# Splits of peer_u between the HGRN heads' steps, modulation rows as products on TensorE, one-hot gate products in fp32

## The chip, the core and the metric

The kernel runs on one core of one Trainium2 chip. A core has TensorE (PE in the rows, its weight loads PEld), VectorE (DVE), ScalarE (ACT), GpSimd (POOL) and SyncE (SP), whose queue issues most of the transfers, and 16 DMA engines. Each engine executes its own queue in order. The metric is the device time of one execution in microseconds. Of the kernel before, three executions took 3266.9 to 3286.5 us, their median is 3282.34 us.

## The reference

One layer over 1024 latent tokens of width 1024 and 256 context tokens. Two linear-attention mixers of four heads each run in both directions over the sequence (HGRN2 with a gate per key channel, mLSTM with a stabilised exponential gate); their output goes through a projection, a residual and a layer norm, then through PEER: eight heads of product-key retrieval over 128 x 128 = 16384 experts of one neuron each. Cut to what the change touches:

```python
mod_l = jax.nn.silu(c) @ w_mod[l] + b_mod[l]                 # 6 x 1024 modulation values
sh1_l, sc1_l, g1_l, sh2_l, sc2_l, g2_l = jnp.split(mod_l[:, None, :], 6, axis=-1)
...
x = _affine_ln(ALPHA * x + g1_l * (mix_l @ w_out[l]), ln1_g[l], ln1_b[l])
h = _modulate(x, sh2_l, sc2_l)
# PEER, per token: the gates of its 8 x 16 best experts, idx = key0 * 128 + key1
act = gelu(jnp.einsum('pd,ped->pe', h, u_tab[idx]))
y = jnp.einsum('pe,ped->pd', gate * act, v_tab[idx])
x = _affine_ln(ALPHA * x + g2_l * y, ln2_g[l], ln2_b[l])
```

## The kernel before

The kernel is one program in stages. A scheduler puts the instructions of each engine in an order by its own model of their durations; the code's order is only the starting point, so an instruction written in one stage may stand in an earlier one, as far as buffers allow. In order of time:

- **0 to 85 us**: the modulation columns of the first layer norm, the layer norm, and its transposed output `xmT` as a pair of fp16 and bf16 (a value and its remainder). All large products are three passes of such pairs.
- **85 to 550 us, HGRN** (`hgrn`): gates of the mLSTM, the values `v`, then four heads in two directions, eight calls of `one()`. One call projects the gate (`sg`, `kr`), makes a scan on VectorE (L398), decayed keys and queries (`kh`, `kt`, `qt`, `qe`), transposes `kh` into `km` through the PSUM tile `tr` (L428; `tr` has two buffers), and then makes the states `S` chunk by chunk (L449, L451) and the outputs. In the same stretch `modrows` makes four rows of 1024 modulation values that are wanted later: for each of 11 blocks of 384 columns, eight loads `wm` of w_mod and a multiply (L682) or multiply-add (L684) on VectorE, 128 partitions wide; the sums over the partitions are left to `modsums` (L697, a product with ones, after the last head).
- **550 to 950 us, mLSTM** and the readout: VectorE carries convolutions (L550, L552) and decay matrices (L615).
- **950 to 1157 us, mix_out**: output projection, layer norm, the query projection for part of the tokens.
- **1157 to 1490 us**: scores against the keys and top-k.
- **1490 to 2003 us, gate tiles**: five tiles of 128 tokens (640 tokens, the "dense" ones) get a matrix of 16384 gates per token, by products of one-hot rows, in 160 quads of four tokens each (`gate_tile`, L1045 to L1056).
- **2003 to 3275 us, final stage**: for each of 128 second keys, `dense_s` takes the product of all 640 tokens with 128 experts' u rows (L1147), `dense_w` applies gelu and gates, `dense_y` multiplies with the v rows (L1180). The other three tiles of tokens gather their experts' rows by indirect transfers (`Gather`, L1088), with a VectorE dot product (L1107) or accumulation (L1115) for each row; these run beside all stages from 1157 on.

Two things tie the stages. **Splits**: `peer_u`, transposed, is needed as a pair of fp16 or bf16 value and remainder. `g.uprep(m)` makes m of the 128 parts: SP loads 512 KB into `us` (L195), ScalarE casts it (L198), GpSimd subtracts (L199), SP stores 512 KB to the DRAM tile `Ud` (L202). They are spread over the stages as filling; `us` and `uT` have two buffers each. **Spilled tiles**: `dense_s` of 60 of the 128 parts (`NPRE`) is done ahead, in the scoring and gate stages, and its result goes to DRAM (`Sd`, 320 KB) and is loaded again in the final stage.

## Time and profile before

| what | value |
| --- | --- |
| median of three runs | 3282.34 us |
| profiled execution: time, span | 3277.14 us, 3275.3 us |
[...]
| busy share: PE, DVE, POOL, ACT | 90%, 86%, 57%, 38% |
| chain that ended last: PE, DVE, DMA, issue | 38%, 32%, 13%, 9% |
| HBM traffic | 274 GB/s over the span |

The profile is of one execution. A busy share is a mean over all stages, so it tells which engine leads but not what a stage waits for; the rows below give it by stage. The chain that ended last is followed back from the last instruction, at each step to what released it; a line's share there is the time that it held the end up. "issue" is time in which the engine waited for nothing that the profile shows. In a row such as `uT<-us,uT 128x1024 x7` the output stands left of the arrow.

### The profile page before, as it was taken

What the parts mean: (1) busy time and instruction counts of PE and PEld (TensorE: products, weight loads), DVE (VectorE), ACT (ScalarE), POOL (GpSimd) and SP (SyncE); (2) the same over time, 40 slices, a digit from 0 to 9 for tenths busy, and PEclk for the clock granted to TensorE, in tenths of its full rate; (3) what the DMA queues carried; (4) which work ended last, traced back from release to release, by engine and by line L of the source; (5) the groups of instructions that cost most, each with busy time, mean ns of one, the idle gap of its engine ahead of it and who ended that gap; (6) DMA issues with size and microseconds to landing.
All of it is one profiled execution on the core that took longest, in us unless ns stands there. A gap on an engine that the chain in (4) does not pass through costs nothing.

```text
span 3275.3 us, 51376 instructions
## 1 busy us (share of the span) xinstructions
PE 2947.6 (90%) x18685; PEld 1911.1 (58%) x18831; DVE 2821.4 (86%) x5605; ACT 1231.1 (38%) x1869; POOL 1853.5 (57%) x1358
## 2 busy tenths in 40 slices
PE   7888789787889889999999987999999999999997
PEld 3644456465777666667777764555555555555553
DVE  8478774889878999999998887889998999889999
ACT  3464462334435442226667663212222122222222
POOL 3555563552236636535555665666676666666665
PEclk8888887898999999999999987999999999999998
DMA  7676664651147659876889789999999999999994
GB/s 287 223 249 224 219 223 160 208 185 52 46 158 253 227 202 351 299 288 213 286 276 309 260 265 363 342 338 362 359 341 365 355 361 360 370 365 360 359 357 181
DMA packets 328626, 900.63 MB, mean 275 GB/s; under 512 B 29084, under 2 KB 121252, under 8 KB 320436
## 3 DMA queue, kind: packets, MB, share of 16 engines
q1 hardware_dynamic: 217780, 494.64, 42.8%
q0 software_dynamic: 110592, 402.70, 33.8%
q8 instruction: 147, 2.41, 0.3%
q14 instruction: 107, 0.88, 0.1%
HBM read 758.80 MB, written 138.43 MB: 274 GB/s over the span
## 4 chain that ended last, share of the span: by engine, by line
PE 38%; DVE 32%; DMA 13%; issue 9%; POOL 4%; ACT 3%; SPq 0%; DVEq 0%; POOLq 0%; ACTq 0%
PE y L1180 14%; PE S L1147 12%; DMA row<-in_peer_v_dram,idx 3%; DVE us L1107 3%; DVE mz L552 2%; PE pj L230 2%; DVE hg L1115 2%; DMA row<-in_peer_u_dram,idx 2%; DMA us<-in_peer_ut_dram 2%; DMA uT<-Ud 2%; DVE mra L684 2%; PE y L1054 2%; PE y L1055 2%; POOL row L1088 1%; DMA wm<-in_w_mod_dram 1%
## 5 line engine op out<-in xcount | busy, mean ns | idle before, releaser
L1147 PE MATMUL S<-hTd,uT 128*128 128x320 f16 (+1 forms) x6144 | 912.7, 303 | 19.7 <-DMA uT<-Ud 11.1
L1180 PE MATMUL y<-vs,w 128*128 128x512 bf16 x3726 | 860.7, 380 | 21.8 <-DVE ya L1187 7.7
L1147 PEld LDWEIGHTS <-uT 128*128 128x128 bf16 x6144 | 608.5, 99 | 292.3 <-DMA uT<-Ud 14.6
L1180 PEld LDWEIGHTS <-w 128*128 128x128 bf16 x3840 | 376.0, 98 | 441.8 <-issue 23.0
L1088 POOL DMA_INDIRECT row<-in_peer_u_dram,idx x384 | 389.4, 1014 | 269.0 <-DVE us L1107 136.9
L1115 DVE SCALAR_TENSOR_TENSOR hg<-row,dot,hg 128x1024 f32<-128x1024 f32 x381 | 488.5, 1282 | 35.5 <-DMA row<-in_peer_v_dram,idx 32.2
L1088 POOL DMA_INDIRECT row<-in_peer_v_dram,idx x384 | 397.2, 1034 | 208.9 <-DVE hg L1115 103.6
L1107 DVE SCALAR_TENSOR_TENSOR us<-row,hg 128x1024 f32<-128x1024 f32 x384 | 465.0, 1211 | 40.4 <-DMA row<-in_peer_u_dram,idx 36.4
L199 POOL TENSOR_TENSOR uT<-us,uT 128x1024 bf16<-128x1024 f32 x128 | 305.8, 2394 | 254.5 <-ACT uT L198 226.3
L1152 ACT ACTIVATE ge<-S 128x320 f32<-128x320 f32 x256 | 114.0, 446 | 546.5 <-PE S L1147 544.9
L222 PE MATMUL pj<-xmT,wb 128*128 128x512 f16 (+3 forms) x1216 | 270.2, 377 | 30.0 <-ACT pad L542 19.8
L1046 POOL TENSOR_TENSOR kT<-kT,eT 128x512 bf16<-128x512 bf16 x160 | 176.3, 1115 | 207.5 <-DVE kT L1045 118.0
L1163 POOL TENSOR_TENSOR vs<-row,vs 128x1024 bf16<-128x1024 f32 x128 | 274.0, 2141 | 33.4 <-ACT vs L1162 31.0
L1162 ACT CAST vs<-row 128x1024 bf16<-128x1024 f32 x128 | 133.4, 1043 | 339.6 <-DMA row<-in_peer_v_dram 327.5
L230 PE MATMUL pj<-wb,xmT 128*128 128x256 f16 (+1 forms) x1728 | 227.3, 291 | 26.2 <-DVE rsg L755 16.6
L1187 DVE TENSOR_TENSOR ya<-ya,y 128x512 f32<-128x512 f32 x310 | 207.8, 680 | 27.6 <-PE y L1180 26.7
L230 PEld LDWEIGHTS <-xmT 128*128 128x128 f16 (+1 forms) x1968 | 187.2, 104 | 75.4 <-issue 34.3
L222 PEld LDWEIGHTS <-wb 128*128 128x128 f16 (+1 forms) x1248 | 127.1, 104 | 153.6 <-issue 52.4
L198 ACT CAST uT<-us 128x1024 bf16<-128x1024 f32 x128 | 132.9, 1043 | 189.2 <-DMA us<-in_peer_ut_dram 177.4
L1054 PE MATMUL y<-kT 128*128 128x128 bf16 x640 | 159.5, 295 | 31.2 <-DVE kT L1047 22.5
L1050 ACT ACTIVATE kT<-kT,gf 128x128 bf16<-128x128 bf16 x320 | 148.7, 570 | 98.5 <-PE y L1054 56.9
L1056 ACT COPY gst<-y 128x512 f32<-128x512 f32 x160 | 178.3, 1123 | 11.6 <-PE y L1055 11.6
(399 smaller groups left out, 4408.6 us busy)
## 6 DMA issues: line engine op xcount, KB each, us to landing
us<-in_peer_ut_dram SPq DMA_DIRECT2D x128, 512.0 KB, 5.2
Ud<-uT SPq DMA_DIRECT2D x128, 512.0 KB, 2.9
uT<-Ud SPq DMA_DIRECT2D x128, 512.0 KB, 7.0
row<-in_peer_v_dram SPq DMA_DIRECT2D x128, 512.0 KB, 7.1
Gd<-gst SPq DMA_DIRECT2D x20, 1984.0 KB, 13.6
Gt<-Gd SPq DMA_DIRECT2D x31, 1280.0 KB, 11.2
Sd<-ge SPq DMA_DIRECT2D x60, 320.0 KB, 8.8
kT<-Sd SPq DMA_DIRECT2D x60, 320.0 KB, 8.7
```

Source lines behind the costliest of these rows:

```text
L199: nc.gpsimd.tensor_tensor(lo, uf, hi, op=OP.subtract)
L222: g.nc.tensor.matmul(ps[:, :t1 - t0], w.t[a][:, k, c0:c0 + 128], g.xmT[b][:, k, t0:t1], start=(k == 0 and a == b), stop=(k == KD - 1 and a ...
L230: g.nc.tensor.matmul(ps, g.xmT[a][:, k, t * 128:(t + 1) * 128], w.t[b][:, k, :w.n], start=(k == 0 and a == b), stop=(k == KD - 1 and a == 1))
L1054: nc.tensor.matmul(o, oh[:, 2, :, i], oh[:, 0, :, i], start=True, stop=False)
L1056: nc.scalar.copy(gs[:, :, q * 4:q * 4 + 4].rearrange("p e t -> p t e"), ps.rearrange("p (t e) -> p t e", e=128))
L1088: d = g.nc.gpsimd.indirect_dma_start(out=b, out_offset=None, in_=self.I["peer_u" if n < 128 else "peer_v"][0], in_offset=bass.IndirectOffs ...
L1107: nc.vector.scalar_tensor_tensor(g.gscr, b, 1.0, self.ps, op0=OP.mult, op1=OP.mult, accum_out=dot[:, j:j + 1])
L1115: nc.vector.scalar_tensor_tensor(self.ps, b, dot[:, j:j + 1], self.ps, op0=OP.mult, op1=OP.add)
L1147: m = nc.tensor.matmul(ps[:, :hn], uT[:, a, k, :], g.hTd[b][:, k, i * hn:(i + 1) * hn], start=(k == 0 and (a, b) == (0, 0)), stop=(k == KD ...
L1163: nc.gpsimd.tensor_tensor(v[:, 1], vf, v[:, 0], op=OP.subtract)
L1180: nc.tensor.matmul(ps, w[:, a, t * 128:(t + 1) * 128], v[:, b, h * 512:(h + 1) * 512], start=(n == 0), stop=(n == 3 * GI - 1))
L1187: nc.vector.tensor_add(ya, ya, ps)
```

## The change

Four parts.

1. **Splits.** The calls of `g.uprep` move: none is left in the mLSTM, its readout and after the heads; 8 stand after each of the two blocks of HGRN values, and 10 inside each `one()` (3 between the gate projections, 3 between the transposes, 4 between the states). 32 stay in mix_out. `uT` gets a third buffer.
2. **Modulation rows.** VectorE's multiplications and `modsums` go. The rows are now products on TensorE, with the conditioning column `cs` as the stationary operand and 512 columns of w_mod streaming: one row of output each, in four different quarters (32 partitions) of the PSUM tile `tr`, in two halves of four rows. The loads `wm` are 32 of 512 KB. A `tr` buffer is held until its half is summed.
3. **Buffers of the last stages.** `score` takes its staging from `us` in place of `uf`; `dense_s` has three `uT` buffers; the dot product L1107 writes its unused product over its own input row.
4. **Gate tiles.** A quad had two compares, a VectorE, a GpSimd and two ScalarE multiplications in bf16, and eight bf16 products on operands with a step of four elements. It now has two compares, a GpSimd multiplication into fp32, written 512 bytes apart from element to element, a ScalarE copy into fp32, and four fp32 products on contiguous operands. `NPRE` rises from 60 to 66.

```diff
@@ Uprep
-            uT = self.pool.tile([128, 2, KD, 128], BF, name="uT")
+            uT = self.pool.tile([128, 2, KD, 128], BF, name="uT", bufs=3)
@@ hgrn
         inputs(0)
+        g.uprep(8)
         inputs(1)
+        g.uprep(8)
...
                 nc.scalar.activation(kr[:, t0:t1], ps, AF.Sigmoid, scale=-1.0)
+                g.uprep(1)
...
                 nc.scalar.copy(km[:, t0:t0 + n, :], pt[:, :n * 128].rearrange("p (t k) -> p t k", k=128))
+                g.uprep(1)
...
                         states(4 + 8 * n + 4 * (i // 2 if d == 0 else 1 - i // 2))
+                        g.uprep(1)
...
                     one(2 * hh + e, d, w, qs[e])
-                    g.uprep(4)
@@ modrows
-            for k in range(KD):
-                wt = mp.tile([128, CW], F32, name="wm", bufs=2)[:, 0:n]
...
-                nc.vector.scalar_tensor_tensor(acc, wt, g.cs[:, k:k + 1], acc, op0=OP.mult, op1=OP.add)
+    for h in range(2):
+        bb = mp.tile([128, 512], F32, name="bb")
...
+        ps = g.pp.tile([128, 512], F32, name="tr", bufs=2)
         for k in range(KD):
+            for x in range(2):
+                wt = mp.tile([128, 1024], F32, name="wm", bufs=2)
+                c = 2 * D + h * 2048 + x * 1024
+                nc.sync.dma_start(wt, I["w_mod"][0, k * 128:(k + 1) * 128, c:c + 1024])
+                for i in range(2):
+                    q = 2 * x + i
+                    nc.tensor.matmul(ps[32 * q:32 * q + 1], g.cs[:, k:k + 1], wt[:, i * 512:(i + 1) * 512],
+                                     start=(k == 0), stop=(k == KD - 1))
+        for q in range(4):
...
+            nc.vector.scalar_tensor_tensor(bb[o], ps[o], 1.0 if r == 2 else 0.0, bb[o], op0=OP.add, op1=OP.add)
+            nc.sync.dma_start(g.mrow[r:r + 1, (n % 2) * 512:(n % 2 + 1) * 512], bb[o])
@@ gate_tile
-            nc.vector.tensor_tensor(oh[:, 1], g.iob, col(0), op=OP.is_equal)
-            nc.gpsimd.tensor_tensor(oh[:, 3], oh[:, 1], col(3), op=OP.mult)
-            nc.vector.tensor_tensor(oh[:, 0], g.iob, col(1), op=OP.is_equal)
-            nc.vector.tensor_tensor(oh[:, 2, :, 2:], oh[:, 1, :, 2:], col(2)[:, :, 2:], op=OP.mult)
-            for i in range(2):
-                nc.scalar.activation(oh[:, 2, :, i], oh[:, 1, :, i], AF.Copy, scale=gf[:, t0 + i:t0 + i + 1])
+            for a in range(2):
+                nc.vector.tensor_tensor(cm[:, a], g.iob, eT[:, a, None, t0:t0 + 4].to_broadcast([128, 128, 4]), op=OP.is_equal)
+            nc.gpsimd.tensor_tensor(oh[:, 0].rearrange("p t e -> p e t"), cm[:, 0], gf[:, None, t0:t0 + 4].to_broadcast([128, 128, 4]), op=OP.mult)
+            nc.scalar.copy(oh[:, 1], cm[:, 1].rearrange("p e t -> p t e"))
...
-                nc.tensor.matmul(o, oh[:, 2, :, i], oh[:, 0, :, i], start=True, stop=False)
-                nc.tensor.matmul(o, oh[:, 3, :, i], oh[:, 0, :, i], start=False, stop=True)
+                nc.tensor.matmul(ps[:, i * 128:(i + 1) * 128], oh[:, 0, i], oh[:, 1, i], start=True, stop=True)
@@ Gather
-            nc.vector.scalar_tensor_tensor(g.gscr, b, 1.0, self.ps, op0=OP.mult, op1=OP.mult, accum_out=dot[:, j:j + 1])
+            nc.vector.scalar_tensor_tensor(b, b, 1.0, self.ps, op0=OP.mult, op1=OP.mult, accum_out=dot[:, j:j + 1])
@@ dense_s
-    uT = g.up.tile([128, 2, KD, 128], BF, name="uT")
+    uT = g.up.tile([128, 2, KD, 128], BF, name="uT", bufs=3)
@@ constants
-NPRE = 60
+NPRE = 66
```

How the scheduler's order changes is shown at three places. The first is GpSimd at the end of the HGRN and the start of the mLSTM: `qe` (L422, after the change L425) belongs to the last HGRN head, L77 splits weights of the mLSTM, `kw` is its first own operation. Before:

```order
L422 TENSOR_TENSOR qe<-q,qe 128x1024
L199 TENSOR_TENSOR uT<-us,uT 128x1024 x7
L77 TENSOR_TENSOR wb_4674<-wf,wb_4673 128x2048
L199 TENSOR_TENSOR uT<-us,uT 128x1024 x4
L77 TENSOR_TENSOR wb_5276<-wf,wb_5275 128x2048
L199 TENSOR_TENSOR uT<-us,uT 128x1024 x6
L77 TENSOR_TENSOR wb_5928<-wf,wb_5927 128x2048
L199 TENSOR_TENSOR uT<-us,uT 128x1024 x2
L586 TENSOR_TENSOR kw<-mkm,gcol 128x1280
L199 TENSOR_TENSOR uT<-us,uT 128x1024 x3
```

And with the change, at the same place:

```order
L425 TENSOR_TENSOR qe<-q,qe 128x1024
L199 TENSOR_TENSOR uT<-us,uT 128x1024 x10
L77 TENSOR_TENSOR wb_4787<-wf,wb_4786 128x2048
L199 TENSOR_TENSOR uT<-us,uT 128x1024 x4
L77 TENSOR_TENSOR wb_5293<-wf,wb_5292 128x2048
L199 TENSOR_TENSOR uT<-us,uT 128x1024 x6
L77 TENSOR_TENSOR wb_5873<-wf,wb_5872 128x2048
L589 TENSOR_TENSOR kw<-mkm,gcol 128x1280 x2
L647 TENSOR_TENSOR acm<-acm,tm 128x2x128 x2
```

72 splits stand ahead of this `qe` before and 76 after; behind it there were 28 up to the end of the mLSTM, nine of them behind the first `kw`, and now there are 20, all ahead of it.

The second place is the first HGRN heads. On VectorE, before (L398 is a head's scan, L406, L420, L421 and L419 its keys and queries, L468 the masked scores):

```order
L682 TENSOR_SCALAR mra<-wm,cs 128x384
L684 SCALAR_TENSOR_TENSOR mra<-wm,cs,mra 128x384 x3
L398 SCALAR_TENSOR_TENSOR sg<-rs,sg 128x1280
L406 TENSOR_TENSOR qt<-sg 128x1024
L684 SCALAR_TENSOR_TENSOR mra<-wm,cs,mra 128x384 x2
L420 SCALAR_TENSOR_TENSOR kt<-kr,oml,kt 128x1024
L421 TENSOR_TENSOR qt<-q,qt 128x1024
L684 SCALAR_TENSOR_TENSOR mra<-wm,cs,mra 128x384
L419 SCALAR_TENSOR_TENSOR kh<-kr,oml,kh 128x1280
```

With the change (L401, L409, L422 to L424 and L472 are the same steps, L404 the scan of a backward head, L453 the first state of a head):

```order
L401 SCALAR_TENSOR_TENSOR sg<-rs,sg 128x1280
L409 TENSOR_TENSOR qt<-sg 128x1024
L423 SCALAR_TENSOR_TENSOR kt<-kr,oml,kt 128x1024
L424 TENSOR_TENSOR qt<-q,qt 128x1024
L404 SCALAR_TENSOR_TENSOR sg<-rs,sg 128x1280
L409 TENSOR_TENSOR qt<-sg 128x1024
L692 SCALAR_TENSOR_TENSOR bb<-tr,bb 1x512 x4
L453 COPY S<-up 128x128
L455 SCALAR_TENSOR_TENSOR S<-S,dec,ob 128x128
```

The accumulations are gone from between the steps; three heads' scans and the four additions of the first half of the rows stand ahead of the first state. On TensorE, with the change, the products of the rows stand ahead of the first head's transposes (L431, `kh`), which are written into the PSUM buffer that the first half (`tr_989`) leaves; `pj_2800` is a gate projection:

```order
L222 MATMUL pj_2800<-xmT0_108,wb1_2471 128x512
L686 MATMUL tr_989<-wm_1046,cs_123 1x512 x2
L686 MATMUL tr_989<-wm_1050,cs_123 1x512 x2
L686 MATMUL tr_1067<-wm_1068,cs_123 1x512 x2
L431 MATMUL tr_2009<-ident_81,kh_1999 128x128 x4
L686 MATMUL tr_1067<-wm_1072,cs_123 1x512 x2
```

Before, a projection stood directly ahead of these transposes, and the gate projections of later heads behind them; now those of four heads stand ahead.

The third place is TensorE at the end of the gate tiles. Before, the last quads' products (L1054, L1055) follow each other, and the next dense tile (L1147) stands behind the last of them:

```order
L1055 LDWEIGHTS kT
L1055 MATMUL y<-kT 128x128
L1147 LDWEIGHTS uT
L1147 MATMUL S<-hTd_8036,uT 128x320
```

With the change the last quad (L1039) stands in the middle of a dense tile (L1131):

```order
L1131 LDWEIGHTS uT
L1131 MATMUL S<-hTd_7813,uT 128x320
L1039 MATMUL y<-kT 128x128 x8
L1131 LDWEIGHTS uT
L1131 MATMUL S<-hTd_7813,uT 128x320
L1131 LDWEIGHTS uT
L1131 MATMUL S<-hTd_7814,uT 128x320
```

In units of one dense tile, 26.5 stand ahead of the eighth quad before and 66.4 ahead of the first product of the final stage (L1180); with the change it is 27.7 and 71.0.

## Rows read from the trace of the kernel before

**Rows 1.** busy by stage: length, PE, PEld, DVE, ACT, POOL; PEclk, DMA share, GB/s

```profile
143.00:528.00 385.00, 321.93 (x1683) 194.91 (x1703) 269.40 (x301) 198.58 (x238) 221.36 (x96) 0.84 0.66 224
528.00:950.00 422.00, 339.95 (x2273) 247.65 (x2284) 344.09 (x707) 149.99 (x197) 149.86 (x64) 0.88 0.39 132
950.00:1157.00 207.00, 179.11 (x1367) 140.27 (x1366) 175.09 (x540) 99.77 (x157) 122.36 (x70) 0.95 0.67 230
1157.00:1490.00 333.00, 305.30 (x2273) 222.19 (x2273) 318.49 (x1439) 93.96 (x172) 149.37 (x150) 0.97 0.76 274
1490.00:1947.00 457.00, 431.25 (x3348) 344.36 (x3346) 411.78 (x961) 313.30 (x567) 274.74 (x255) 0.97 0.85 275
1947.00:1982.00 35.00, 17.91 (x124) 13.38 (x123) 32.74 (x55) 25.94 (x46) 27.39 (x26) 0.54 0.89 286
...
2003.00:3252.00 1249.00, 1231.47 (x6682) 665.36 (x6795) 1132.14 (x1395) 281.09 (x396) 832.07 (x658) 1.00 0.93 352
```

**Rows 2.** chain of waits by line, 85 to 550 us, 950 to 1157 us

```profile
by line: DVE mra L684 12.7%; issue 8.9%; DMA wm<-in_w_mod_dram 8.6%; DMA us<-in_peer_ut_dram 6.1%; PE oa L480 5.4%; PE pj L230 5.3%; PE pj L222 4.6%; PE oa L477 3.6%; PE ob L440 3.2%; DVE qt L406 3.1%; PE up L440 3.1%; DVE S L451 2.7%; PE s
...
by line: PE pj L842 13.8%; DMA us<-in_peer_ut_dram 12.1%; POOL uT L199 8.1%; issue 7.1%; DMA wqf<-in_peer_wq_dram 6.4%; DVE mz L851 3.9%; POOL uT L77 3.7%; PE oa L918 3.7%; DVE lnst L145 3.0%; DVE ind L889 2.6%; DVE cnt L951 2.6%; DVE mh L8
```

**Rows 3.** L199's subtractions by stretch: length, POOL busy (count), PEclk, DMA share, GB/s

```profile
0.00:85.00 85.00, 15.82 (x7) 0.87 0.76 288
85.00:200.00 115.00, 45.10 (x19) 0.92 0.68 237
200.00:528.00 328.00, 117.10 (x48) 0.83 0.63 214
528.00:750.00 222.00, 65.53 (x28) 0.87 0.55 186
```

**Rows 4.** timeline of SP's queue: two loads of splits, two splits apart

```profile
93.64 0.43 SPq L195 DMA_DIRECT2D us<-in_peer_ut_dram  x1
...
103.71 0.38 SPq L195 DMA_DIRECT2D us<-in_peer_ut_dram  x1
```

**Rows 5.** what SP's queue waited for, 157 to 530 us: us, times, longest

```profile
SPq L202 <- POOL uT L199: 80.3, 19, 18.0
...
SPq L680 <- DVE mra L684: 60.3, 35, 6.2
```

**Rows 6.** groups by line (second: 1490 to 1947 us): busy us, mean ns | idle before

```profile
L552 DVE SCALAR_TENSOR_TENSOR mz<-pad,cwT,mz 128x1024 f32<-128x1024 f32 x64 | 98.8, 1554 | 0.7
...
L1056 ACT COPY gst<-y 128x512 f32<-128x512 f32 x144 | 160.7, 1123 | 11.2 <-PE y L1055 11.1
```

**Rows 7.** pieces of the chain of waits: start us, us, what

```profile
549.88 0.95 PE tr L697 x2
...
2965.19 6.52 PE S L1147 x48
```

**Rows 8.** single lines: ns min/median/max, first and last start us, forms

```profile
L684 DVE SCALAR_TENSOR_TENSOR mra<-wm,cs,mra x77: 472/1454/4420, 164.9 to 466.3; 128x384 f32<-128x384 f32 x70, 128x256 f32<-128x256 f32 x7
...
L552 DVE SCALAR_TENSOR_TENSOR mz<-pad,cwT,mz x64: 1251/1277/5079, 592.8 to 810.5; 128x1024 f32<-128x1024 f32 x64
...
L428 PE MATMUL tr<-ident,kh x80: 272/273/475, 212.7 to 512.7; 128*128 128x128 f32 x80
...
L1046 POOL TENSOR_TENSOR kT<-kT,eT x160: 1032/1052/2162, 1491.8 to 1978.8; 128x512 bf16<-128x512 bf16 x160
...
L574 ACT COPY mkm<-tr x12: 363/574/599, 656.1 to 829.0; 128x512 f32<-128x512 f32 x8, 128x256 f32<-128x256 f32 x4
```

**Rows 9.** timeline of the gate stage: start us, us, engine, line

```profile
1702.76 0.29 PE L1054 MATMUL y<-kT 128*128 128x128 bf16 x1 [0.62 <-DVE kT L1048]
...
1703.02 0.40 DVE L1045 TENSOR_TENSOR kT<-iob,eT 128x512 bf16<-128x512 bf16 x1
...
1703.10 0.30 PE L1055 MATMUL y<-kT 128*128 128x128 bf16 x1
...
1703.77 1.35 DVE L1045 TENSOR_TENSOR kT<-iob,eT 128x512 bf16<-128x512 bf16 x1
```

## What is predicted, and why

> **What bounds the kernel now.** I read the table by stages first: in each stretch, which engine is busy nearly all the time? From 2003 us to the end it is TensorE, 1231 of 1249 us; while experts are scored (1157 to 1490) it is VectorE, 318 of 333; in the mLSTM no engine is full but VectorE leads with 344 of 422. The gate stage (1490 to 1947) has TensorE at 431 of 457, and then 56 us in which TensorE is busy for 26 [rows 1]. The HGRN stretch, 143 to 528, is nobody's: TensorE 322 of 385, VectorE 269, and its granted clock is 0.84 [rows 1]. So there I read the chain of waits by line: the accumulation of the modulation rows (L684) is its largest line with 12.7%, the loads `wm` behind it have 8.6%, the loads of the splits 6.1% [rows 2]. The splits run through all of it: 48 from 200 to 528, one per 6.8 us [rows 3]. When nothing is in their way two of them, on two `us` buffers, take 10.1 us, 5.0 each [rows 4]. What holds them back is the shared queue of SP: it stood 60 us waiting for L684 and 80 us for the subtractions of the splits [rows 5], and all later transfers stand behind it.
>
> **The change, part by part.** The profiled execution has a span of 3275.3 us and a time of 3277.1, 5 us under the median of 3282.3; the sum is made against 3277.1.
>
> *Modulation rows.* 77 accumulations, 112 us of VectorE at a median of 1.45 us, go [rows 8], with 11 first multiplies and 56 of 88 loads (the bytes stay the same). In their place TensorE takes 64 products of one output row by 512 columns. The trace has that shape in the old sums, 0.95 us for the two records of one [rows 7]: 61 us in all if they run one after the other; the four quarters of the array might overlap, which no row here shows, and at twice the speed it is 30. TensorE's 322 us become 352 to 383. The eight old sums stood on the chain one by one, 8 x 0.95 = 7.6 us, and go wholly: **-8**.
>
> *Splits to the HGRN heads.* The order on GpSimd shows that the planner had pulled most of them there already: 72 stand before the last head's `qe` now, 76 then. 26 (7 and 19) are through at 200 us [rows 3], so 50 must follow. At the undisturbed 5.2 us (the pair at 10.1 and a little for the weight splits) that takes 260 us, at today's 6.8 us 340, against 328: bounds -68 and +12. With L684 gone SP waits less, so the middle, 6.0, would give -28. But TensorE with 352 to 383 us must fit too, and it now has 63 us idle of 385; a stage of 365 us leaves it nearly none. I take **-20**.
>
> *mLSTM.* 20 splits instead of 28 fall here [rows 3], and all before the first `kw`. L552 shows what a split costs VectorE: 1277 ns at the median, 1554 in the mean [rows 6, 8], 64 x 0.28 = 18 us of stalls, since the two engines take turns. Eight of 28 fewer: 8/28 x 18 = **-5**. Nothing (all off the chain) and -18 (none left beside L552) are the bounds.
>
> *mix_out.* 32 splits instead of 28. The splits' loads and subtractions have 20% of the chain of this 207 us stretch [rows 1, 2], 42 us for 28, 1.5 each: 4 x 1.5 = **+6**. Hidden wholly it is 0, at full cadence 4 x 6.0 = +24.
>
> *Scoring.* One `us` buffer takes the place of two `uf`, and a third `uT` is there. VectorE at 318 of 333 us covers this: **0**. Writing the dot product back over `row` in place adds no element to L1107: 0, unless the gather that reuses the row comes later; it waits for L1107 today already.
>
> *Gate tiles.* A quad of tokens now has 3.17 us (457 over the 144 evacuations L1056 of that stretch [rows 6]). What goes per quad: one VectorE multiply, two ScalarE ones, and eight matmuls, of which three pitches take 0.34 us (1702.76 to 1703.10), 0.9 for eight [rows 9]. What comes: four fp32 products of 128 columns, each a quarter of the 0.95 us of one with 512 [rows 7], together 0.95; a ScalarE copy that reads with a step; and a GpSimd multiply that writes with a step of 512 bytes. For the copy the nearest rows are L574, 0.57 us contiguous, and L1056, 1.12 us writing with a step [rows 6, 8]. Two ScalarE instructions go for this one, and ScalarE, at 313 of 457, has room for either: 0. The multiply is 1.05 us now [rows 8] and I take it as unchanged, nearest to itself, the risk being the third rival. By the order 3.4 more dense tiles are made in this stage. One takes 6.52 us of TensorE for 48 of its products, nearly the tile [rows 7]: +22. TensorE is idle for 26 + 17 = 43 us from 1490 to 1982 [rows 1], much of it for handshakes of a quad that now has fewer of them. So the 22 fit in: **-5**, bounds -25 (half the idle time closed and no more work) and +60 (nothing closed, and the third `uT` brings loads earlier into a DMA share of 0.85).
>
> *Final stage.* 71.0 tiles of 128 stand before its first product in the order, 66.4 today: 4.6 fewer to make here, 4.6 x 6.52 = 30 us of a TensorE that is busy for 98.6% [rows 1, 7]. A spilled tile is read back as 320 KB where a made one reads 512, so DMA, at 0.93, doesn't grow. I take **-27**; 0 if transfers, at 0.93 [rows 1], set the pace instead.
>
> Sum: -8 - 20 - 5 + 6 + 0 - 5 - 27 = -59, so **3218 us**.
>
> **The rivals.** *First: the heads start late.* In the order all 16 products of the first half of the modulation rows, and its four additions, stand ahead of the first head's transposes and first state. Those transposes start at 212.7 us now and the eighth head's last one at 512.7, 43 us per head [rows 8]. The half needs 16 loads of 512 KB, on SP between some 14 splits: at 6.0 us from 165 us on, where the first accumulation is now [rows 8], they end near 250. The heads then start 38 us late. Against this: projections of four heads run in that time, and VectorE has less to do per head. If the 43 us stay, HGRN gives +38 instead of -20: 3218 + 58 = **3276**, no change. It decides from a pace of 6 us per split and a head period above 38 us.
>
> *Second: the whole chain share of the modulation rows comes free.* 12.7% + 8.6% of 465 us [rows 2] are 99 us, less some 30 of new products: -69 instead of -20, **3169**. For it speaks that SP waited 60 us for L684 [rows 5]; against it that another chain stands close behind, TensorE's.
>
> *Third, on the other side: the strided multiply.* On ScalarE a step between written fp32 elements makes 1.12 us out of 0.57 [rows 6, 8], a factor of two. On GpSimd it would make 2.1 us out of 1.05. The two engines take turns, too: a compare that takes 0.40 us alone took 1.35 beside a multiply [rows 9]. So a quad costs GpSimd 2.1, two compares 0.8, and gathers 0.8 (275 us less 144 x 1.05, over 144, a little rounded down since some multiplies were held up to 2.16 us [rows 1, 8]), 3.7 us together instead of 3.17: (3.7 - 3.17) x 144 = 76, and some 11 for the last 16 quads, which now take 35 us [rows 1] and would take 16 x 2.9 with their gathers done. The gate stage gives +87 instead of -5: **3310**, slower than before. It decides when the multiply passes 1.55 us. [...]
>
> **How the numbers follow.** A measurement of this kernel tells about 1% from no change, so faster means under 3249 and slower over 3315. Forecast 0.49 (its own range 3185 to 3249); late heads 0.23; the full share 0.12; strided multiply 0.16, half of it with late heads beside it, which is 3310 + 58 and slower. Faster: 0.49 + 0.12 = 0.61. Same: 0.23 + 0.08 = 0.31. Slower: 0.08. The range goes from 3165, just under the second rival, to 3295, which takes in the first and leaves out the third.
>
> **What would show it.** HGRN: the last state products end near 520 us instead of 542, splits run at 6 us, and SP's queue no longer waits for a VectorE line of the modulation rows. If the first transposes come at 250 and the last after 550, the first rival is right. Products: TensorE's records of one row by 512 lie 0.24 us apart if quarters overlap, 0.47 if not. mLSTM: the mean of L552 nears its median. Gate stage: the multiply stays at 1.05 us; at 2.1 the third rival is right and GpSimd is over 90% busy from 1490 on. Final stage: some 1222 us long, TensorE still full. The sum would be wrong altogether if the final stage keeps its 1249 us, because then transfers and not TensorE set its end.

## The result, and the profile after

The changed kernel takes **3223.3 us** at the median (four runs, 3221.3 to 3223.9), the kernel before 3277.1 us in the runs made beside it; the ratio is 0.984, with a 95% interval from 0.982 to 0.986. The forecast was 3218 us, in a range from 3165 to 3295, and faster by over 1% with a chance of 0.61. So the total came out as forecast. Its parts did not, as the stages show: two errors cancelled.

The profiled execution has a span of 3221.9 us instead of 3275.3, and a mean granted TensorE clock of 0.953 of full speed instead of 0.938. On its page, the first line gives busy us (share of the span) and instructions of each engine, the second the chain that ended last, by engine:

```profile
PE 2938.5 (91%) x18943; PEld 1892.4 (59%) x18943; DVE 2611.8 (81%) x5352; ACT 1181.8 (37%) x1699; POOL 1846.0 (57%) x1358
...
PE 42%; DVE 24%; DMA 11%; POOL 9%; issue 9%; ACT 4%; SPq 0%; DVEq 0%; POOLq 0%; ACTq 0%
```

VectorE has 210 us less to do and its part of the chain fell from 32% to 24%; TensorE has as much work as before in a shorter span, and GpSimd's part of the chain rose from 4% to 9%.

To compare stages I use the first and the last start of a line that marks their borders: the HGRN stretch ends with the last output product of a head, mix_out runs from the first to the last projection product, the gate stage begins with the first GpSimd multiplication of a quad, the final stage with the first y product and ends with the last. Rows of single lines, with min/median/max ns and first and last start in us, of the kernel before (the gate stage's first start, 1491.8, is in [rows 8]):

```profile
L480 PE MATMUL oa<-S,qe x256: 272/323/477, 234.1 to 543.6; 128*64 128x128 f32 x128
...
L842 PE MATMUL pj<-wo,mT x768: 272/273/418, 949.7 to 1116.8; 128*128 128x256 f16 x128, 128*128 128x256 bf16 x64
...
L1180 PE MATMUL y<-vs,w x3726: 375/379/635, 2003.2 to 3251.9; 128*128 128x512 bf16 x197
```

and of the changed kernel (L431 are the transposes of `kh`, L485 the output products, L833 the projection, L1035 and L1036 a quad's multiplication and copy, L1164 the y products):

```profile
L431 PE MATMUL tr<-ident,kh x80: 272/328/476, 254.8 to 487.8; 128*128 128x128 f32 x80
...
L485 PE MATMUL oa<-S,qe x256: 272/323/476, 261.8 to 518.3; 128*64 128x128 f32 x128
...
L833 PE MATMUL pj<-wo,mT x768: 269/273/421, 886.6 to 1055.9; 128*128 128x256 f16 x128, 128*128 128x256 bf16 x64
...
L1035 POOL TENSOR_TENSOR kT<-us,gf x160: 1062/1120/1859, 1448.7 to 1908.0; 128x512 f32<-128x512 bf16 x160
...
L1036 ACT CAST kT<-us x160: 637/670/738, 1449.0 to 1907.5; 128x512 f32<-128x512 bf16 x160
...
L1164 PE MATMUL y<-vs,w x3840: 376/379/634, 1934.4 to 3184.8; 128*128 128x512 bf16 x192
```

| stage | before, us | after, us | difference | predicted |
| --- | --- | --- | --- | --- |
| to the end of HGRN | 543.6 | 518.3 | -25 | -20 |
| then to mix_out (sums, mLSTM) | 406.1 | 368.3 | -38 | -8 - 5 |
| mix_out | 167.1 | 169.3 | +2 | +6 |
| scoring, to the first quad | 375.0 | 392.8 | +18 | 0 |
| gate stage, to the first y product | 511.4 | 485.7 | -26 | -5 |
| final stage, to the last y product | 1248.7 | 1250.4 | +2 | -27 |
| tail | 23.4 | 37.1 | +14 | 0 |
| sum | 3275.3 | 3221.9 | -53 | -59 |

The stages as a table of windows of the changed kernel (length, busy us and instructions of PE, PEld, DVE, ACT and POOL, then the granted clock, the DMA share and GB/s), to be laid beside [rows 1]:

```profile
143.00:518.00 375.00, 341.87 (x1918) 191.12 (x1915) 173.44 (x232) 203.29 (x243) 237.84 (x103) 0.91 0.70 245
518.00:887.00 369.00, 311.69 (x2203) 236.49 (x2203) 308.47 (x685) 135.43 (x183) 124.07 (x52) 0.91 0.34 112
887.00:1056.00 169.00, 154.11 (x1224) 123.12 (x1223) 136.42 (x423) 83.57 (x130) 102.16 (x60) 0.98 0.68 237
1056.00:1449.00 393.00, 345.96 (x2521) 248.75 (x2520) 358.15 (x1566) 115.11 (x207) 176.62 (x166) 0.94 0.75 270
1449.00:1934.00 485.00, 458.51 (x3630) 371.21 (x3629) 385.20 (x857) 307.05 (x461) 304.60 (x287) 0.99 0.90 301
1934.00:2836.00 902.00, 899.58 (x4994) 489.46 (x4994) 800.16 (x1043) 204.58 (x293) 596.74 (x474) 1.00 0.95 358
2836.00:3222.00 386.00, 317.51 (x1584) 156.66 (x1581) 343.39 (x376) 74.50 (x101) 239.74 (x186) 0.92 0.82 303
```

In the HGRN stretch VectorE has 173 us instead of 269, and TensorE fills 342 of 375. In the gate stage VectorE falls to 385 us of 485, and TensorE is full, 459. The last two rows show the surprise: up to 2836 us TensorE is busy all the time, and in the last stretch it is not. Here is that stretch up to the last y product, and the same length in the kernel before, in this order:

```profile
2836.00:3185.00 349.00, 317.38 (x1584) 156.66 (x1581) 316.45 (x339) 66.06 (x89) 219.32 (x178) 0.97 0.89 326
2905.00:3252.00 347.00, 345.29 (x1862) 184.48 (x1888) 320.11 (x344) 74.33 (x105) 226.51 (x176) 1.00 0.90 336
```

TensorE idles for 32 us where it idled for 2. The final stage has 57.0 dense tiles for TensorE instead of 61.6, and it isn't shorter; something else now ends last.

### The profile page after: what moved, and what is told of

Its sections match the earlier page's. It is cut to its first block, busy times and chain, and to the rows that moved or that the text cites. A ratio compares the mean times of both kernels' runs of the same rounds, so it can differ in the third digit from the quotient of the medians.

```text
span 3221.9 us, 50811 instructions
## 1 busy us (share of the span) xinstructions
PE 2938.5 (91%) x18943; PEld 1892.4 (59%) x18943; DVE 2611.8 (81%) x5352; ACT 1181.8 (37%) x1699; POOL 1846.0 (57%) x1358
## 3 DMA queue, kind: packets, MB, share of 16 engines
q8 instruction: 149, 2.44, 0.3%
## 4 chain that ended last, share of the span: by engine, by line
PE 42%; DVE 24%; DMA 11%; POOL 9%; issue 9%; ACT 4%; SPq 0%; DVEq 0%; POOLq 0%; ACTq 0%
PE y L1164 16%; PE S L1131 12%; DMA row<-in_peer_v_dram,idx 5%; POOL row L1072 4%; DVE row L1091 3%; PE pj L222 3%; DVE mz L555 3%; PE pj L230 2%; DVE us L1034 2%; POOL vs L1147 2%; DMA us<-in_peer_ut_dram 2%; DMA row<-in_peer_u_dram,idx 2%; DVE hg L1099 2%; POOL uT L199 2%; PE y L1039 1%
## 5 line engine op out<-in xcount | busy, mean ns | idle before, releaser
L1164 PE MATMUL y<-vs,w 128*128 128x512 bf16 x3840 | 878.9, 382 | 40.5 <-POOL vs L1147 16.6
L1131 PE MATMUL S<-hTd,uT 128*128 128x320 f16 (+1 forms) x6144 | 898.6, 300 | 10.7 <-issue 6.2
L1131 PEld LDWEIGHTS <-uT 128*128 128x128 bf16 x6144 | 602.6, 98 | 276.0 <-issue 13.2
L1164 PEld LDWEIGHTS <-w 128*128 128x128 bf16 x3840 | 378.2, 98 | 471.4 <-issue 61.4
L1099 DVE SCALAR_TENSOR_TENSOR hg<-row,dot,hg 128x1024 f32<-128x1024 f32 x381 | 489.5, 1285 | 110.3 <-DMA row<-in_peer_v_dram,idx 94.7
L1072 POOL DMA_INDIRECT row<-in_peer_v_dram,idx x384 | 387.4, 1009 | 219.7 <-DVE hg L1099 133.2
L1091 DVE SCALAR_TENSOR_TENSOR row<-row,hg 128x1024 f32<-128x1024 f32 x384 | 458.7, 1211 | 58.1 <-DMA row<-in_peer_u_dram,idx 52.1
L199 POOL TENSOR_TENSOR uT<-us,uT 128x1024 bf16<-128x1024 f32 x128 | 303.9, 2379 | 188.7 <-ACT uT L198 173.1
L1147 POOL TENSOR_TENSOR vs<-row,vs 128x1024 bf16<-128x1024 f32 x128 | 277.9, 2171 | 28.7 <-ACT vs L1146 23.1
L1035 POOL TENSOR_TENSOR kT<-us,gf 128x512 f32<-128x512 bf16 x160 | 178.3, 1137 | 200.3 <-DVE us L1034 175.5
L222 PE MATMUL pj<-xmT,wb 128*128 128x512 f16 (+3 forms) x1248 | 262.5, 367 | 19.9 <-ACT pad L545 18.5
L1171 DVE TENSOR_TENSOR ya<-ya,y 128x512 f32<-128x512 f32 x310 | 207.3, 681 | 26.1 <-PE y L1164 24.3
L1040 ACT COPY gst<-y 128x512 f32<-128x512 f32 x160 | 171.3, 1075 | 83.9 <-PE y L1039 66.0
L1034 DVE TENSOR_TENSOR us<-iob,eT 128x512 bf16<-128x512 bf16 x320 | 172.4, 588 | 14.6 <-ACT kT L1036 9.0
L1039 PE MATMUL y<-kT 128*128 128x128 f32 x1280 | 165.2, 281 | 17.1 <-ACT kT L1036 8.1
```

The source lines that it names most:

```text
L199: nc.gpsimd.tensor_tensor(lo, uf, hi, op=OP.subtract)
L222: g.nc.tensor.matmul(ps[:, :t1 - t0], w.t[a][:, k, c0:c0 + 128], g.xmT[b][:, k, t0:t1], start=(k == 0 and a == b), stop=(k == KD - 1 and a ...
L1034: nc.vector.tensor_tensor(cm[:, a], g.iob, eT[:, a, None, t0:t0 + 4].to_broadcast([128, 128, 4]), op=OP.is_equal)
L1039: nc.tensor.matmul(ps[:, i * 128:(i + 1) * 128], oh[:, 0, i], oh[:, 1, i], start=True, stop=True)
L1072: d = g.nc.gpsimd.indirect_dma_start(out=b, out_offset=None, in_=self.I["peer_u" if n < 128 else "peer_v"][0], in_offset=bass.IndirectOffs ...
L1091: nc.vector.scalar_tensor_tensor(b, b, 1.0, self.ps, op0=OP.mult, op1=OP.mult, accum_out=dot[:, j:j + 1])
```

## The experiments

All times are medians, beside the kernel before on the same chip; where there is no interval, it is one execution. This table gives the stages of all of them by the same marks (us), ahead of the single accounts. "Rows", "splits", "buffers" and "gate" are the four parts of the change.

| kernel | HGRN | to mix | mix | score | gate | final | tail | median us |
| --- | --- | --- | --- | --- | --- | --- | --- | --- |
| before | 544 | 406 | 167 | 375 | 511 | 1249 | 23 | 3277 |
| changed | 518 | 368 | 169 | 393 | 486 | 1250 | 37 | 3223 |
| e1 rows alone | 523 | 371 | 167 | 373 | 517 | 1251 | 24 | 3224 |
| e2 splits alone | 547 | 391 | 171 | 377 | 514 | 1250 | 23 | 3277 |
| e3 gate alone | 540 | 399 | 171 | 389 | 514 | 1255 | 23 | 3289 |
| e4 changed, 60 spilled | 519 | 368 | 170 | 378 | 477 | 1241 | 33 | 3189 |
| e5 buffers alone | 544 | 398 | 167 | 371 | 496 | 1242 | 32 | 3251 |
| e6 changed, 270 gathers | 516 | 364 | 170 | 382 | 496 | 1210 | 23 | 3161 |
| e7 60 spilled, 270 gathers | 520 | 368 | 169 | 377 | 499 | 1262 | 21 | 3209 |
| e8 a third of y left out | 520 | 365 | 170 | 378 | 481 | 1287 | 43 | 3247 |
| e9 as e8, half of v loaded | 520 | 368 | 167 | 388 | 486 | 1248 | 47 | 3226 |
| e10 as e8, half accumulations | 522 | 365 | 171 | 392 | 478 | 1274 | 42 | 3244 |
| e11 72 spilled, 290 gathers | 522 | 368 | 170 | 390 | 519 | 1176 | 28 | 3169 |
| e12 e4 with the old gate tiles | 523 | 368 | 169 | 388 | 494 | 1243 | 33 | 3220 |

One thing is to be read off it first. The scheduler orders each kernel anew, so a stage that an edit doesn't touch can move: the scoring stage lies between 371 and 393 us with no clear cause in the edit, and the stretch to mix_out of the gate tiles alone and of the buffers alone is 7 or 8 us shorter than before although neither touches it. e8 and e10, whose edits lie behind the scoring, differ there by 14 us. Differences under some 15 us in the scoring stage, and under some 10 in another, are not assigned to an edit here.

### e1: the modulation rows alone

```diff
-            for k in range(KD):                                   # 88 loads, 88 VectorE operations
-                wt = mp.tile([128, CW], F32, name="wm", bufs=2)[:, 0:n]
...
-                modsums(g, I)
+    for h in range(2):                                            # 32 loads, 64 products on TensorE
+        ps = g.pp.tile([128, 512], F32, name="tr", bufs=2)
```

> The kernel before with the modulation rows alone moved to TensorE (the old sums gone), splits and gate tiles as before. Theory A, the accumulations on VectorE and the small loads behind them held the HGRN heads up: the HGRN stretch ends 25 us earlier, at about 519 us instead of 544, the sums' 8 us go too, the total is 33 us less, 3244 us. Theory B, the gain of the HGRN stretch comes from where the splits stand: only the 8 us of the sums go, 3269 us.

It took 3223.5 us, ratio 0.983 (0.982 to 0.985): the rows alone are worth as much as the whole change. HGRN is 21 us shorter, the stretch behind it 35. In the kernel before, SP's view from 157 to 530 us has, beside [rows 5], one more long line for the loads of the rows (us, times, longest):

```profile
SPq L680 <- DVE S L451: 71.7, 27, 8.2
```

So these loads waited for VectorE for more than twice the 60 us that the prediction counted. What SP's queue waits for in e1 in the same stretch:

```profile
SPq L202 <- POOL uT L199: 210.6, 56, 11.7
...
SPq L685 <- PE tr L688: 34.4, 21, 2.5
```

The accumulations are gone from this queue, and of VectorE some 11 us of small waits are left; it now waits for the splits' subtractions, 211 us, and for the products of the rows, 34. The splits now wait mostly for their own chain of load, cast and subtraction: 56 come from 200 us to the end of the heads, one per 5.8 us, against 6.9 before. So theory A, and more than it gave: of the 22 us over it nearly all lie behind the heads. This edit takes two things away at once, the waits in SP's queue and 112 us of VectorE's work; no run parts them.

### e2: the splits alone

```diff
         inputs(0)
+        g.uprep(8)
...
                 nc.scalar.activation(kr[:, t0:t1], ps, AF.Sigmoid, scale=-1.0)
+                g.uprep(1)
...
-            g.uprep(4)        # mLSTM and readout: all calls out
```

> The kernel before with the splits alone moved (16 after the values, 80 inside the heads, none in mLSTM and readout; two uT buffers as before). Theory A, splits are only filling in the HGRN stretch and do harm beside VectorE in the mLSTM: with 8 fewer behind the heads the mLSTM gains some 20 us and the HGRN stretch, which still has the accumulations on VectorE, loses as much, 3277 us within 8. Theory B, the place of the splits carries the gain: 3250 us or less.

3276.9 us, ratio 1.001 (0.999 to 1.002): nothing. Its subtractions by stretch (length, POOL busy and count, ...), 200 us to the end of the heads, and from there to mix_out, and a line of SP's waits from 157 to 530 us:

```profile
200.00:547.00 347.00, 123.29 (x52) 0.82 0.64 217
...
547.00:938.00 391.00, 45.88 (x19) 0.91 0.35 118
...
SPq L680 <- DVE mra L684: 64.0, 33, 6.2
```

52 splits in the first stretch, 6.7 us each, against 50 up to the end of the heads in the kernel before. Moving the calls into the heads moves two splits. With L684 still in SP's way they come hardly faster. The stretch behind the heads is 15 us shorter, of which e3 and e5 show 7 to 8 without any such edit; the HGRN and mix_out together lose 8. Theory A holds: the named part of the change, the place of the splits, is worth nothing by itself.

### e3, e5, e12: gate tiles and buffers, apart and together

e3 changes `gate_tile` and its operands (with the dot product in place, since the freed buffer holds the one-hots), e5 the buffers without it, e12 is the changed kernel with the old `gate_tile` and 60 spilled tiles.

```diff
 e3
-            nc.gpsimd.tensor_tensor(oh[:, 3], oh[:, 1], col(3), op=OP.mult)
...
+            nc.gpsimd.tensor_tensor(oh[:, 0].rearrange("p t e -> p e t"), cm[:, 0], gf[:, None, t0:t0 + 4].to_broadcast([128, 128, 4]), op=OP.mult)
+            nc.scalar.copy(oh[:, 1], cm[:, 1].rearrange("p e t -> p t e"))
 e5
-    uT = g.up.tile([128, 2, KD, 128], BF, name="uT")
+    uT = g.up.tile([128, 2, KD, 128], BF, name="uT", bufs=3)
```

> The kernel before with the gate tiles alone changed (two compares, one GpSimd multiplication, one ScalarE copy, four fp32 products; 60 spilled tiles as before). Theory A, a quad now has fewer handshakes and less VectorE work: the gate stage is some 25 us shorter and the rest unchanged, 3252 us. Theory B, the gate stage is set by TensorE, whose work per quad is the same: 5 us, 3272 us.

> The kernel before with the buffers of the last stages alone changed (staging of the scores from us, three uT buffers, dot product in place), old gate tiles, 60 spilled tiles. The gate tiles alone lost 10 us, and in the whole change the gate stage is 26 to 35 us shorter. Theory A, the buffers carry this: with a third uT the next dense tile is there when the quads leave TensorE free, the gate stage ends 30 us earlier, 3248 us. Theory B, it needs both, since the old quads wait for each other and not for uT: less than 8 us from the kernel before, 3271 us or more.

> The changed kernel with 60 spilled tiles and with the old gate tiles, all else (rows, splits, buffers) changed. With the new gate tiles and 60 tiles it took 3189 us, the rows alone 3224; the gate tiles alone lost 10 us and the buffers alone gained 22. Theory A, the new gate tiles help only where a third uT feeds TensorE between the quads: without them the gate stage is some 19 us longer (496 against 477), 3205 to 3212 us. Theory B, the buffers carry it all and the new gate tiles are worth nothing or a loss: 3180 to 3193 us.

The gate tiles alone: 3288.6 us, ratio 1.003 (1.001 to 1.004), a little slower. The buffers alone: 3250.5 us, ratio 0.993 (0.991 to 0.996). The changed kernel with 60 spilled tiles takes 3188.9 us with the new gate tiles (e4) and 3219.9 with the old ones (e12). So the same edit loses 10 us with the old buffers and gains 31 with the new ones (and the new rows and splits, which lie stages ahead). Of the 31, 17 lie in the gate stage and 10 in the scoring, which the edit doesn't touch; 3219.9 is above the 3205 to 3212 of theory A. The buffers alone came near the 3248 of their theory A in the total, but with 15 us of the 30 expected in the gate stage. There, against the kernel before, the quads alone give +3 us, the buffers alone -15 and both (e4) -34: neither carries it alone. TensorE's waits for the next tile's `uT` in the gate stage show why. In e3 (us, times, longest):

```profile
PEld L1139 <- DMA uT<-Ud: 40.9, 12, 8.2
...
PE S L1139 <- DMA uT<-Ud: 36.8, 11, 7.9
```

and in the kernel before:

```profile
PEld L1147 <- DMA uT<-Ud: 9.3, 4, 4.1
...
PE S L1147 <- DMA uT<-Ud: 8.1, 4, 3.8
```

The lighter quads ask for the next dense tile earlier, and with two `uT` buffers its 512 KB have not landed: 41 us of waits for the weight loads instead of 9. In the changed kernel and in e12, with three buffers, the view lists no such wait. With the buffers alone (496 us) VectorE has 448 us of a 495 us stage, and TensorE waits for the operands of the old quads instead, as in this line of e5:

```profile
PEld L1055 <- ACT kT L1051: 29.7, 23, 3.1
```

With the quads alone (514 us) it waits for the loads; with both the stage takes 477 us. The gains of the parts don't add up over the whole kernel: e12 has the new rows, splits and buffers and is, at 3220 us, hardly below the 3224 of the rows alone.

### e4, e6, e7, e11: what the spilled tiles and the gathers are worth

```diff
 e4
-NPRE = 66
+NPRE = 60
 e6
-G2 = 240
+G2 = 270
 e7
-NPRE = 66
+NPRE = 60
-G2 = 240
+G2 = 270
 e11
-NPRE = 66
+NPRE = 72
-G2 = 240
+G2 = 290
```

`G2` is the number of gathers ahead of the final stage; 768 are needed in all.

> The changed kernel with 60 spilled tiles instead of 66. Theory A, the final stage lasts as long as its 521 gathers, 2.35 us each, whatever TensorE has to do: six tiles more there change nothing, the scoring and gate stages get a little shorter, 3215 to 3225 us. Theory B, the one of the prediction, TensorE sets the final stage: 6 x 6.5 = 39 us more there and up to 20 less before it, 3243 us or more.

> The changed kernel with 30 more gathers ahead of the final stage (270 instead of 240, spread over the gate tiles). Theory A, the final stage is as long as the longer of two things: its TensorE work (6.52 us for each of 57 dense tiles left and 3840 products of 0.219 us, 1213 us) and its gathers (2.33 us each, and 25 us at the end). In the changed kernel 521 gathers give 1240, so TensorE waits; with 491 they give 1169 and TensorE sets 1213: 37 us less there, up to 10 more in the gate stage, 3190 to 3200 us. Theory B, gathers just run as slowly as the program lets them, at the pace of the dense tiles: the final stage stays at 1250, the total at 3223 or above.

> The changed kernel with 60 spilled tiles and 270 gathers ahead. Theory A: TensorE has 61 tiles left, 1240 us, and sets the final stage; the 30 gathers moved ahead gain nothing, 3185 to 3200 us. Theory B, gathers alone set the final stage: 30 x 2.33 = 70 us less, 3130 us.

> The changed kernel with both loads of the final stage moved ahead further: 72 spilled tiles and 290 gathers. With 66 and 270 TensorE set the final stage, 1210 us. Theory A: TensorE has 52 tiles and the products left, 1180 us, the 471 gathers take 1122 us: the final stage is 30 us shorter, but the stages ahead, whose TensorE and DMA are full at 0.97, grow by the same: 3150 to 3170 us, no clear difference to 3161. Theory B, there is still room in the gate stage: 3140 us or less.

e4 took 3188.9 us, ratio 0.973 (0.971 to 0.975): with six tiles *fewer* made ahead the kernel is 34 us faster than the changed one. Its y products:

```profile
L1164 PE MATMUL y<-vs,w x3713: 376/379/634, 1911.8 to 3153.2; 128*128 128x512 bf16 x196
```

They take 1241 us, 9 less than in the changed kernel, though 61 dense tiles stand among them instead of 57. This is TensorE's sum by the pieces of [rows 7] and 0.219 us for a y product (46 of them take 10.09 us in the chain of waits of the kernel before): 61.2 x 6.52 + 3840 x 0.219 = 1240 us. In the changed kernel that sum is 57 x 6.52 + 841 = 1213, and the stage takes 1250. So there TensorE isn't what ends last. Theory A of this run had the gathers alone set the stage and the total unchanged; it missed the 15 us less in the scoring and 9 each in the gate and final stages.

e6 took 3161.1 us, ratio 0.967 (0.962 to 0.971). Its y products, and of its windows the gate stage and a part of the final one:

```profile
L1164 PE MATMUL y<-vs,w x3727: 376/379/634, 1927.6 to 3137.8; 128*128 128x512 bf16 x197
```

```profile
1449.00:1934.00 485.00, 461.70 (x3640) 371.70 (x3640) 411.78 (x828) 304.66 (x457) 331.37 (x310) 0.98 0.97 336
...
2563.00:2963.00 400.00, 397.41 (x2145) 213.51 (x2182) 356.87 (x473) 87.36 (x123) 268.78 (x214) 1.00 0.96 364
```

With 30 gathers more ahead the final stage takes 1210 us. It has 55.2 dense tiles, fewer than the changed kernel, so TensorE's sum is 1201, and TensorE idles for 19 us in the stage, as it did before (17), where it idles for 34 in the changed kernel. The price in the gate stage is 10 us, where DMA now stands at 0.97. The 3161 us are below the 3190 to 3200 of theory A, since the tail is 14 us shorter too and the scoring 11. e7, with the same gathers but 60 tiles, took 3209.5 (0.977 to 0.985 of before) and a final stage of 1262 us: moving 30 gathers off it gives nothing where TensorE has 1240 us to do. Theory A gave 1240; the 22 us over it go with waits of the y products for VectorE's additions that free their PSUM buffers (L1171), 4 us in e4 and here (us, times, longest):

```profile
PE y L1164 <- DVE ya L1171: 23.7, 21, 2.8
```

So the longer of two loads, TensorE's and the gathers', is the least that the final stage takes, and the change took from one of them only. How long the gathers alone would take can't be read from their pace in a stage that TensorE fills: it is there the stage divided by its gathers, 2.32 us in the kernel before. Where TensorE idles, from 2836 us on in the changed kernel, 141 gathers come every 2.30 us, and the last y product starts 24 us behind the last of them. By that the 523 of the kernel before take 1227 us, an estimate, beside TensorE's 1243: the two were nearly even. For the changed kernel the same estimate gives 1222, and the stage took 1250, so the gathers' pace is no constant; what makes it is asked by e8 to e10.

e11 moves both further: final stage 1176 us, where 1180 were expected, and the gate stage 519. Total 3168.9, ratio 0.966 (0.963 to 0.968), no gain over e6: of the 34 us taken from the final stage 23 come back in the gate stage, and the rest in the scoring, the tail and the HGRN. e6 is faster than both kernels of this case: 0.967 of the kernel before, where the changed one is at 0.984.

### e8, e9, e10: what paces the gathers

```diff
 e8
-        for a, b in PASSES:
+        for a, b in PASSES[:2]:
 e9, besides
-    nc.sync.dma_start(vf, I["peer_v"][0].rearrange("(a b) d -> a b d", b=128)[:, i2, :])
+    nc.sync.dma_start(vf[:, :512], I["peer_v"][0].rearrange("(a b) d -> a b d", b=128)[:, i2, :512])
 e10, besides e8
+                h = slice(0, 512)
-                nc.vector.scalar_tensor_tensor(self.ps, b, dot[:, j:j + 1], self.ps, op0=OP.mult, op1=OP.add)
+                nc.vector.scalar_tensor_tensor(self.ps[:, h], b[:, h], dot[:, j:j + 1], self.ps[:, h], op0=OP.mult, op1=OP.add)
```

> The changed kernel with one of the three passes of the last product left out, 1280 of its 3840 products, so 280 us of TensorE less in the final stage and the outputs without that pass. Theory A: the gathers set the final stage of the changed kernel already, so it stays between 1225 and 1255 us. Theory B, TensorE sets it: it shortens by 100 us or more.

> The kernel with a third of the last products left out (its final stage of 1287 us is set by the gathers, 2.44 us each), and now with only half of each v tile loaded and used twice: 33 MB less of some 430 MB in the final stage, engines' work unchanged. Theory A, the gathers' pace is that of the DMA engines, busy 0.93: 8% fewer bytes make the final stage 60 to 95 us shorter, 1190 to 1225 us. Theory B, the pace is that of VectorE and of the rows' buffers that it frees: unchanged, over 1265 us.

> The kernel with a third of the last products left out, and with the accumulation of gathered v rows on half the columns only: of some 260 of these in the final stage each is some 0.6 us shorter, 160 us less of VectorE, transfers unchanged; the outputs of three tiles of tokens lack half. Theory A, DMA sets the gathers' pace: the final stage stays within 25 us of 1287. Theory B, VectorE does: 1130 to 1200 us.

e8 takes 280 us off TensorE, and its final stage is not shorter but longer, 1287 us. Its y products and a window of the stage:

```profile
L1164 PE MATMUL y<-vs,w x2467: 376/379/634, 1914.8 to 3202.0; 128*128 128x512 bf16 x190
```

```profile
2163.00:2563.00 400.00, 321.02 (x1640) 168.21 (x1668) 338.34 (x397) 80.78 (x117) 249.68 (x204) 0.89 0.93 344
```

TensorE is busy for 321 of 400 us and its granted clock is 0.89; DMA is at 0.93, as over the final stage before [rows 1]. The gathers come every 2.44 us, 521 x 2.44 = 1271. That TensorE doesn't set this stage is shown; that it became 37 us longer than the changed kernel's was not expected and isn't explained.

e9, with 33 MB less to load, took 1248 us, 39 less than e8; expected were 60 to 95 if DMA set the pace, and under 22 if not, so neither theory holds as stated. e10, with 133 us less of VectorE in the stage (160 were expected), took 1274, 14 less. So the length of VectorE's accumulations doesn't set the gathers' pace; transfers seem to have a part, by one execution of each kernel; and neither explains the whole 2.4 us. That part stays open.

## Why the prediction was right, and where it was not

**HGRN, -20 against -25: the mechanism and its size were right.** The middle cadence of 6.0 us per split came out as 318 us for 55 splits, 5.8, as the subtractions by stretch show (200 to 518 us, and 518 to 887):

```profile
200.00:518.00 318.00, 135.09 (x55) 0.91 0.68 235
...
518.00:887.00 369.00, 39.59 (x16) 0.91 0.34 112
```

SP's queue lost its long VectorE lines, as in e1 (us, times, longest, from 157 to 530 us):

```profile
SPq L202 <- POOL uT L199: 214.8, 58, 11.1
...
SPq L683 <- PE tr L686: 39.0, 18, 4.5
```

But the prediction entered this term under the splits' place. e1 and e2 show that the place is nothing: it is the rows that let the splits run faster, wherever they are written.

**The late heads, the first rival, began as it said and didn't cost.** The first transposes start at 254.8 us, where 250 was worked out and 212.7 was before. TensorE's timeline (start, us, engine, line) shows the pairs of products with four records in 1.03 us, and the last ones of the half directly ahead of the transposes, the first state behind:

```profile
171.55 1.03 PE L686 MATMUL tr<-wm,cs 128*1 128x512 f32 x4
172.50 1.04 PE L222 MATMUL pj<-xmT,wb 128*128 128x512 f16 x4
...
253.04 1.87 PE L686 MATMUL tr<-wm,cs 128*1 128x512 f32 x4 [3.74 <-DMA wm<-in_w_mod_dram]
...
254.85 1.12 PE L431 MATMUL tr<-ident,kh 128*128 128x128 f32 x4
...
259.60 0.29 DVE L453 COPY S<-up 128x128 f32<-128x128 f32 x1 [7.41 <-PE ob L444]
```

The point that decides is the other one that the rival named: the period of a head fell from 43 us to (487.8 - 254.8) / 7 = 33, under the 38 from which it is harmless. That VectorE without the accumulations and TensorE with the projections done ahead carry this is argued, not shown.

**The products overlap in the array's quarters.** Two records of different quarters start 0.01 us apart. From a pair's first record to TensorE's next instruction it is 0.95 us, as the first two lines of the timeline above show (171.55 to 172.50). So a product takes 0.48 us instead of the 0.95 of the old sums (both at a granted clock of 1.00), and by that all 64 are some 31 us of TensorE, at the lower bound of the 30 to 61 given.

**Sums and mLSTM, -13 against -38: right in sign, a third of the size.** The two terms are the sums' 8 us and the price of a split, and together they were too small. The price was taken from L552 alone, 18 us of stalls, and L552 has not come nearer its median at all. Groups of the changed kernel (busy us, mean ns | idle before; L555 is the old L552, L618 the old L615):

```profile
L555 DVE SCALAR_TENSOR_TENSOR mz<-pad,cwT,mz 128x1024 f32<-128x1024 f32 x64 | 105.8, 1664 | 0.6
...
L618 DVE SCALAR_TENSOR_TENSOR dm<-bM,gcol,mlm 128x128 f32<-128x128 f32 x64 | 30.0, 510 | 7.1 <-DMA bM<-negM 5.7 <-PE ob L631 1.2
```

and of the kernel before:

```profile
L615 DVE SCALAR_TENSOR_TENSOR dm<-bM,gcol,mlm 128x128 f32<-128x128 f32 x64 | 44.9, 753 | 11.5 <-DMA bM<-negM 9.2 <-PE ob L628 1.2 <-PE oa L628 1.0
```

L555 means 1664 ns where 1554 were; L618 means 510 where 753 were. So VectorE's stalls don't lie in one line; that where a split falls decides which line shows them is argued. VectorE was busy 339 us from 544 to 950 us and is 308 from 518 to 887; for the nine splits fewer in that stretch (16 instead of 25) it is some 3.4 us each, sums and all, not the 0.6 that L552's share gave. e2, which has 19 splits there and keeps the sums, gained 15 of the 38; e1, with 19 and without the sums, 35. So at the same splits 20 us go with the rows and their sums, for which the prediction had 8; no run parts the two terms further.

**mix_out, +6 against +2**, within its bounds.

**Gate tiles, -5 against -26, and the third rival.** The strided multiplication (L1035), whose writes lie 512 bytes apart, takes 1120 ns at the median where the contiguous one took 1052 [rows 8]: 6% and not the double. So the factor of two that ScalarE shows at L1056 doesn't carry over to GpSimd here, and the rival falls. The copy, 670 ns, replaces two of 567. What the prediction missed is that the quad's gain and the third `uT` need each other (e3, e5, e12).

**Scoring, 0 against +18.** No run says why it is longer: with 66 tiles it takes 393 us here and 378 in e8, with 60 tiles 378 in e4 and 388 in e12. What the six tiles cost ahead of the final stage is not settled either: scoring and gate stage together take 879 us in the changed kernel and 859 to 874 in e8 to e10, against 855 in e4; with 270 gathers it is 877 with 66 tiles and 876 with 60. So it is between 1 and 24 us, and whether "the 22 fit in", as the prediction has it, stays open.

**Final stage, -27 against +2 (+15 with the tail): the step that failed outright.** The step was "4.6 x 6.52 = 30 us of a TensorE that is busy for 98.6%": it read the engine's busy share as the cause of the stage's length. The trace of before held a warning, in its chain of waits from 2003 to 3252 us:

```profile
by line: PE y L1180 36.2%; PE S L1147 16.2%; issue 10.7%; DMA row<-in_peer_v_dram,idx 9.2%; DVE hg L1115 4.9%; POOL row L1088 3.8%; DMA row<-in_peer_u_dram,idx 3.4%; POOL vs L1163 2.9%; DVE us L1107 2.5%; DVE ya L1187 2.2%; DVE w L1168 1.9%
```

TensorE's two lines have 52% of it; the gathers with their VectorE operations and their own issue have 24%. The prediction named this case, transfers that set the end, as what would make the sum wrong and kept it as a bound, but it worked out no number for it and made no rival of it. The end of the kernel follows the start of the last gather by 58 us before and by 61 after; the row of the last gathers in the changed kernel, and in the one before:

```profile
L1072 POOL DMA_INDIRECT row<-in_peer_v_dram,idx x384: 935/942/1767, 1481.3 to 3160.9; - x192
```

```profile
L1088 POOL DMA_INDIRECT row<-in_peer_v_dram,idx x384: 932/941/1938, 1524.0 to 3217.7; - x192
```

TensorE's last products wait with them because each v tile takes one of the seven `row` buffers that the gathers use. The waits of the changed kernel from 2836 to 3185 us show the links (us, times, longest):

```profile
PE y L1164 <- POOL vs L1147: 14.9, 7, 3.5
...
PE y L1164 <- ACT vs L1146: 9.2, 3, 6.2
...
ACT vs L1146 <- DMA row<-in_peer_v_dram: 189.9, 26, 11.9
...
SPq L1144 <- DVE hg L1099: 95.7, 26, 6.6
```

The y products wait 24 us for the two halves of a v tile (`vs`), the first half waits for the tile's load, and SP's queue issues that load (L1144) when VectorE's accumulations (L1099) have been done with a buffer.

So 3218 for 3223 is luck, two errors that cancel: 51 us too little gain on the mLSTM, the gate stage and the HGRN and 4 on mix_out, and 61 too much on the scoring, the final stage and the tail.

## What to carry to other kernels

Where a stage is 98% busy on one engine, read the chain of waits over the same stretch before work is taken off that engine: here TensorE was busy for 98.6% and had 52% of the chain. Two loads that are nearly even must be moved together. The two that were moved here, with the rows, splits, buffers and quads new in all four kernels, took these shares of the kernel before: 0.973 with neither load moved (e4), 0.984 with the tiles alone (the changed kernel), 0.981 with the gathers alone (e7), 0.967 with both (e6). What an operation costs its neighbours can exceed its own time on the chain: 88 short accumulations with their loads and sums were worth 55 us, where the prediction had 8 for the sums and 20 for the splits that waited behind them in SP's queue, while moving those splits was worth nothing. How much of the 55 is SP's queue and how much VectorE's time is not shown.

## What the runs showed of the hardware

- Four products with one row of output each, in different quarters of 32 partitions, run in pairs: 0.48 us each at 512 columns of fp32, against 0.95 for one alone in the old sums, both at a granted clock of 1.00.
- GpSimd writing fp32 with 512 bytes between elements took 1.12 us for 128 x 512, against 1.05 for contiguous bf16; ScalarE writing with a step took 1.07 to 1.14 us (medians) against 0.57 contiguous.
- Some VectorE operations took longer beside GpSimd's, others not. In the kernel before, the compares of the quads (L1045, L1047) took 0.41 us at the median where no GpSimd instruction overlaps them and 1.26 where an L1046 does. L552 took 1.25 to 1.29 us alone, and every one above that, up to 5.08, overlaps a GpSimd instruction. The accumulations L1115 took 1.28 us, alone and beside an L1046. So that the two engines take turns, as the prediction says, holds for some lines and not for others; what decides it is not shown.
- With a third of the last products left out TensorE was busy for 321 of 400 us of the final stage and its mean granted clock there was 0.89, against 1.00 in the changed kernel, where it was busy all the time. The gathers came every 2.44 us instead of 2.35 over the stage; why is open.
